# A fused LoRA kernel: 62 of 64 tiles keep a place of their own, and one group's halves go through the engines in turn

## The chip, the cores and the metric

The kernel runs on one NeuronCore of a Trainium2 chip. The metric is the device time of one execution in microseconds (us); the three runs of the kernel before took 124.76, 124.80 and 125.47, median 124.8. A profile is taken of one further execution. Engines are named as in the profile: PE is TensorE (matmuls), PEld its weight loads, DVE is VectorE, ACT is ScalarE, POOL is GpSimd, and SP is SyncE, which here only issues DMA transfers. "Span" is the time from the first to the last instruction in the profile.

## The reference

```python
def setup_inputs():
    batch, seq, d_model, r = 16, 512, 768, 16
    # x: 16 x 512 x 768, A: 768 x 16, B: 16 x 768, all float32; scale = 0.5
...
def reference(x, A, B, scale):
    lora = np.matmul(np.matmul(x, A), B)
    return (x + scale * lora).astype(np.float32)
```

x has 8192 rows (tokens) of 768 numbers, 25.2 MB. Every row is read once, gets a small correction through a rank-16 bottleneck, and is written once. So 50.3 MB cross the memory bus, and A and B are tiny.

## The kernel before

**Tiles.** A tile is 128 tokens, one per partition of the on-chip memory, with 768 float32 each (3 KB per partition, 384 KB in all). There are 64 tiles. `PARTS` cuts them into transfers of 2, 6, 8, 16, 16 and 16 tiles. The on-chip memory holds x in three rooms of 16 tiles (`rooms`), 48 places in all. The tiles of the last part (number 5) are loaded over parts 0, 1 and 2, so they must wait until these have been stored; that load is cut in two halves of 8 tiles, each behind the stores that free its place.

**Groups.** Compute goes in 8 groups of 8 tiles (`GROUP`), each in two halves of 4 (`SUB`). For a group:

1. *Narrow* (line 167): ACT copies the first half to half precision (`xh`), POOL the second half. There are two buffers `xh[0]`, `xh[1]` of a whole group each.
2. *Turn* (line 237): DVE transposes 32 x 32 blocks of `xh` in place, one instruction per half. After that the channel dimension lies along the partitions in every block.
3. *Project* (line 270): PE multiplies by A. 24 matmuls of 128 x 256, with the weights `w_bd` (A repeated on a block diagonal) accumulate `y_ps`, the 16 numbers per token. There are two `y_ps` buffers.
4. *Spread* (line 201): ACT copies four 32-partition blocks of `y_ps`, times the scale, to the diagonal of `y_bd` (two buffers).
5. *Raise* (line 288): PE multiplies by B, a pair of tiles at a time, 4 matmuls per pair (columns 512, 256, 256, 512), into one of two `lora` accumulators.
6. *Add* (line 250): DVE adds a pair's `lora` to the float32 tiles in place.

**Order on the engines.** Every engine runs a program of its own, written inside a block (`nc.Block`, lines 130 to 317). PE's loop takes two groups per turn and weaves the raising of group g with the projection of group g+1 in thirds: raise pairs 0 and 1, project 8 matmuls, raise pair 2, project 8, raise pair 3, project 8. DVE turns both halves of group g+1 and then does the four additions of group g. At start-up DVE also builds `w_bd` from A (lines 216 to 231), and ACT narrows B (`b_half`), which PE spreads with a selection matrix `pick` and ACT copies back as `b_mm`. The scratch for that (`a_rows`, `a_t`, `w_one`, `b_rows`, `b_half`, `pick`) has memory of its own.

**Order of the transfers.** All transfers are issued by SP and run in one queue, in the order of their issue. SP issues the loads of parts 0 and 1, A, B, and parts 2, 3 and 4; then the stores of parts 0, 1 and 2, each once the additions of its groups are done (`s_sum`, which DVE signals after a drain); then the two halves of load 5, the first when the stores of parts 0 and 1 have landed, the second when the store of part 2 has; then the remaining stores.

```python
        for st, done in zip(STORES, (s_out0, s_out0, s_out1)):
            store(st, done)
        e.wait_ge(s_out0, 32)
        load(LOADS[5])
        e.wait_ge(s_out1, 16)
        load(LOADS[6])
        for st in STORES[3:]:
            store(st, s_out)
```

At the end POOL waits until the last stores have landed.

Of the kernel before, what the change touches and what calls it, by code (L numbers as in the profile page):

```python
# [13 lines left out]
PARTS = [2, 6, 8, 16, 16, 16]  # L14

ROOM = [(0, 0), (0, 2), (0, 8), (1, 0), (2, 0), (0, 0)]
# [10 lines left out]
def kernel(  # L27
# [31 lines left out]
    rooms = [sb(f"x_sb{i}", [P, 16, D], fp32) for i in range(3)]  # L59
# [4 lines left out]
    a_rows = sb("a_rows", [P, 64 * R], fp32)  # L64
    a_t = sb("a_t", [P, 2, R, Q], fp32)
    w_one = sb("w_one", [Q, NC, 2, R], MM_DT)
    b_rows = sb("b_rows", [P, D], fp32)
    b_half = sb("b_half", [P, D], MM_DT)
    pick = sb("pick", [P, NQ, Q], MM_DT)
    w_bd = sb("w_bd", [P, NC, 2, P], MM_DT)  # L70
    b_mm = sb("b_mm", [P, D], MM_DT)
    xh = [sb(f"xh{i}", [P, GROUP, D], MM_DT) for i in range(2)]
    y_bd = [sb(f"y_bd{i}", [P, GROUP, P], MM_DT) for i in range(2)]
    lora = [ps(f"lora_ps{i}", [P, 2, D]) for i in range(2)]
    y_ps = [ps(f"ps_yt{i}", [P, GROUP, Q]) for i in range(2)]
# [3 lines left out]
    def sem(name):  # L79
        sems.append(nc.alloc_semaphore(name))  # L80
        return sems[-1]

# [12 lines left out]
    def held(i, s, n):  # L95
        r, s0 = ROOM[i]
        return rooms[r][:, ds(s0 + s, n), :]


    LOADS = [(0, 0, 2), (1, 0, 6), (2, 0, 8), (3, 0, 16), (4, 0, 16), (5, 0, 8), (5, 8, 8)]  # L100
    s_load = {ld: sem(f"s_load{k}") for k, ld in enumerate(LOADS)}

    def load_sem(t):
        i, s = where[t]
        return next(s_load[ld] for ld in LOADS if ld[0] == i and ld[1] <= s < ld[1] + ld[2])

    s_a, s_b = sem("s_a"), sem("s_b")
    s_brows, s_pick, s_bh, s_bp = sem("s_brows"), sem("s_pick"), sem("s_bh"), sem("s_bp")
    s_ready, s_zero, s_bm = sem("s_ready"), sem("s_zero"), sem("s_bm")
    s_nact, s_npool = sem("s_nact"), sem("s_npool")  # L110
    s_turned, s_y, s_spread = sem("s_turned"), sem("s_y"), sem("s_spread")
    s_lora, s_sum = sem("s_lora"), sem("s_sum")

    s_free = [sem(f"s_free{p}") for p in range(PAIRS)]
    s_out0, s_out1, s_out = sem("s_out0"), sem("s_out1"), sem("s_out")

    MMS = 2 * NC
    THIRD = MMS // 3

    STORES = [(0, 0, 2), (1, 0, 6), (2, 0, 8), (3, 0, 16), (4, 0, 16), (5, 0, 8), (5, 8, 8)]  # L120


    def groups_for(i, s, n):
        return where.index((i, s + n - 1)) // GROUP + 1

    STORED = list(dict.fromkeys(groups_for(*st) for st in STORES))
# [3 lines left out]
    programs = ExitStack()  # L130
    block = programs.enter_context(nc.Block(no_gpsimd_drain=True))

    @block.sync
    def _(e):
        def load(ld):
            e.dma_start(out=held(*ld), in_=memory(x2, *ld)).then_inc(s_load[ld], 16)  # L136

        def store(st, done):
            e.wait_ge(s_sum, STORED.index(groups_for(*st)) + 1)
            e.dma_start(out=memory(out2, *st), in_=held(*st)).then_inc(done, 16)  # L140

        load(LOADS[0])
        load(LOADS[1])
        e.wait_ge(s_ready, 1)
        e.dma_start(  # L145
            out=a_rows[0 : NC * APART : APART, :], in_=A.rearrange("(c e) r -> c (e r)", e=64)
        ).then_inc(s_a, 16)
        e.wait_ge(s_brows, 1)
        e.dma_start(out=b_rows[0 : R * APART : APART, :], in_=B).then_inc(s_b, 16)  # L149
        for ld in LOADS[2:5]:  # L150
            load(ld)
        for st, done in zip(STORES, (s_out0, s_out0, s_out1)):
            store(st, done)
        e.wait_ge(s_out0, 32)
        load(LOADS[5])
        e.wait_ge(s_out1, 16)
        load(LOADS[6])
        for st in STORES[3:]:
            store(st, s_out)

    def narrowed(e, copy, done, g, q):
        t = g * GROUP + q * SUB
        for s in dict.fromkeys(load_sem(t + k) for k in range(SUB)):
            e.wait_ge(s, 16)
        if q and g >= 2:
            e.wait_ge(s_y, g - 1)
        copy(  # L167
            out=xh[g % 2][:, ds(q * SUB, SUB), :], in_=held(*where[t], SUB)
        ).then_inc(done, 1)

    @block.gpsimd
    def _(e):
        e.memset(a_rows[0 : NC * APART], 0.0).then_inc(s_ready, 1)  # L173
        e.memset(b_rows, 0.0).then_inc(s_brows, 1)  # L174

        e.sem_inc(s_spread, 1)
        for s in s_free[2:]:
            e.sem_inc(s, 1)
        e.memset(pick, 0.0).then_inc(s_pick, 1)
        e.memset(w_bd.rearrange("p c k m -> p (c k m)").bitcast(fp32), 0.0)  # L180
        for t in y_bd:
            e.memset(t.rearrange("p s m -> p (s m)").bitcast(fp32), 0.0)  # L182
        e.wait_ge(s_pick, 1)
        e.affine_select(  # L184
            out=pick, in_=pick, compare_op=mybir.AluOpType.not_equal, fill=1.0, base=0,
            pattern=[[0, NQ], [-APART, Q]], channel_multiplier=1,
        ).then_inc(s_zero, 1)
        for g in range(NG):
            narrowed(e, e.tensor_copy, s_npool, g, 1)

    @block.scalar
    def _(e):
        e.wait_ge(s_zero, 1)
        e.wait_ge(s_b, 16)
        e.copy(out=b_half, in_=b_rows).then_inc(s_bh, 1)  # L195

        def spread(g):
            e.wait_ge(s_y, g + 1)
            for b in range(NQ):
                q = ds(b * Q, Q)  # L200
                last = e.mul(out=y_bd[g % 2][q, :, q], in_=y_ps[g % 2][q, :, :], mul=sc)  # L201
            last.then_inc(s_spread, 1)

        narrowed(e, e.copy, s_nact, 0, 0)
        e.wait_ge(s_bp, 1)
        e.copy(out=b_mm, in_=lora[0][:, 0, :]).then_inc(s_bm, 1)  # L206
        narrowed(e, e.copy, s_nact, 1, 0)
        for g in range(NG):
            spread(g)
            if g + 2 < NG:  # L210
                narrowed(e, e.copy, s_nact, g + 2, 0)

    @block.vector
    def _(e):
# [13 lines left out]
        e.wait_ge(s_ready, 3)  # L228
        e.wait_ge(s_zero, 1)
        for b in range(NQ):  # L230
            e.tensor_copy(out=w_bd[ds(b * Q, Q), :, :, ds(b * Q, R)], in_=w_one)  # L231

        def turned(g):
            for q, s in ((0, s_nact), (1, s_npool)):
                e.wait_ge(s, g + 1)
                v = xh[g % 2][:, ds(q * SUB, SUB), :].bitcast(fp32)
                last = e.transpose(out=v, in_=v)  # L237
            last.then_inc(s_turned, 1)

        turned(0)  # L240
        for p in range(PAIRS):
            e.wait_ge(s_lora, p + 1)
            e.sem_inc(s_free[p], 1)
        for g in range(NG):
            if g + 1 < NG:
                turned(g + 1)
            for p in range(PAIRS):
                xs = held(*where[g * GROUP + 2 * p], 2)
                e.wait_ge(s_lora, (g + 1) * PAIRS + p + 1)
                ins = e.tensor_tensor(  # L250
                    out=xs, in0=xs, in1=lora[p % 2], op=mybir.AluOpType.add
                )
                if g + 1 < NG or p + 2 < PAIRS:
                    ins.then_inc(s_free[p], 1)
                elif p + 1 == PAIRS:
                    ins.then_inc(s_sum, 1)
            if g + 1 in STORED[:-1]:
                e.drain().then_inc(s_sum, 1)  # L258

    @block.tensor  # L260
    def _(e):


        def projected(h, steps):
            if steps[0] == 0:
                e.wait_ge(s_turned, 1)
            xv = xh[h].rearrange("p s (c j k) -> p s c j k", c=NC, k=2)
            for m in steps:
                c, k = divmod(m, 2)
                last = e.matmul(  # L270
                    y_ps[h], w_bd[:, c, k, :], xv[:, :, c, :, k],
                    start=(m == 0), stop=(m == MMS - 1),
                )
            if steps[0] == 0:
                last.then_inc(s_turned, -1)
            elif steps[-1] == MMS - 1:
                last.then_inc(s_y, 1)

        def raised(h, p):
# [6 lines left out]
            for k in range(2):  # L286
                for n0, w in ((0, 512), (512, 256)) if k == 0 else ((0, 256), (256, 512)):
                    mms.append(e.matmul(  # L288
                        t[:, k, ds(n0, w)], y_bd[h][:, 2 * p + k, :], b_mm[:, ds(n0, w)],
# [4 lines left out]
            mms[1].then_inc(free, -1)  # L294
            mms[-1].then_inc(s_lora, 1)
# [9 lines left out]
        with e.Fori(0, NG // 2):  # L305
            for h in range(2):
                raised(1 - h, 0)
                raised(1 - h, 1)
                projected(h, range(0, THIRD))
                raised(1 - h, 2)  # L310
                projected(h, range(THIRD, 2 * THIRD))
                raised(1 - h, 3)
                projected(h, range(2 * THIRD, MMS))
        for p in range(PAIRS):
            raised(1, p)

    programs.close()  # L317
    nums = [s.num for s in sems]
    assert nums == list(range(nums[0], nums[0] + len(nums))) and sems[-1] is s_out
    nc.gpsimd.sem_clear(range(nums[0], nums[-1]))  # L320
    nc.gpsimd.wait_ge(s_out, 4 * 16)
    nc.gpsimd.sem_inc(s_out, -4 * 16)
# [36 lines left out]
```

## Time and profile before

| | |
|---|---|
| median of three runs | 124.8 us (124.76 to 125.47) |
| the profiled execution's own time | 124.78 us |
| its span | 122.8 us |
| bytes read and written | 25.26 MB and 25.17 MB |
| share of the span in which the 16 DMA engines were busy | 96.7% |
| busiest compute engine: DVE | 85.4 us, 70% of the span |
| PE / ACT / POOL | 47% / 30% / 22% |
| mean granted PE clock | 0.873 |

How to read it: the page of the profile gives shares over the whole span, a strip of 40 slices (each 3.07 us) with the busy tenths of every engine, the granted PE clock and the DMA rate, and then the costliest groups of instructions by line. "Idle before" is the time an engine stood still ahead of instructions of that group, and the arrow names what ended it. The timeline lists instructions in order, with runs of the same instruction merged; its first two columns are the start and the length, in us from the span's start. The profiled execution took 124.78 us, 2.0 more than its span, so a change in the span stands beside the median of 124.8 one to one.

### The profile page before, as it was taken

To read this page: it belongs to the slowest core of one execution; us is meant where nothing else is said; L and a number is where in the kernel's file an instruction comes from. 1 tells how busy PE (TensorE), PEld (TensorE's weight loads), DVE (VectorE), ACT (ScalarE), POOL (GpSimd) and SP (SyncE) were. 2 spreads that over 40 slices of the span, in tenths; PEclk is the share of its full clock that TensorE was granted. 3 is DMA by queue.
4 is the path that set the end of the run, shared out by engine and by line. 5 is a ranking of instruction groups with operands and counts; after the bars stand their busy time and mean duration, and the time that the engine had idled before them with its cause. 6 is when DMAs were issued, how large, how long until landed. Compare 5 with 4: busy or idle time off the path is not lost.

```text
span 122.8 us, 920 instructions
## 1 busy us (share of the span) xinstructions
PE 58.1 (47%) x338; PEld 33.5 (27%) x338; DVE 85.4 (70%) x56; ACT 36.8 (30%) x43; POOL 26.4 (22%) x19
## 2 busy tenths in 40 slices
PE   0000239948907944694584389449439645000000
PEld 0000015625503632362252145235224322000000
DVE  0004984089969999989999998999999859600000
ACT  0002958040199141707604080840400310000000
POOL 7703508000196001707100080440000000000000
PEclk9999999999995999769999958999995999655555
DMA  3999999799799895999999999899799799899990
GB/s 104 434 444 402 424 528 464 304 512 480 304 496 496 384 400 222 466 448 400 480 400 448 440 392 528 384 480 464 336 496 451 336 496 464 344 432 408 472 424 32
DMA packets 2073, 50.44 MB, mean 411 GB/s; under 512 B 252, under 2 KB 252, under 8 KB 536
## 3 DMA queue, kind: packets, MB, share of 16 engines
q1 hardware_dynamic: 2072, 50.43, 96.7%
q14 instruction: 1, 0.01, 0.0%
HBM read 25.26 MB, written 25.17 MB: 411 GB/s over the span
## 4 chain that ended last, share of the span: by engine, by line
DVE 40%; DMA 24%; PE 10%; DVEq 5%; ACT 2%; issue 2%; SPq 2%; POOL 1%; POOLq 0%
DMA x_sb<-in_x_dram 24%; DVE x_sb L250 23%; DVE xh L237 17%; PE lora_ps L288 6%; PE ps_yt L270 4%; DVEq L258 4%; ACT xh L167 2%; DVEq L317 1%; POOL a_rows L173 1%; SPq L145 1%; SPq L136 1%; SPq L149 0%; POOLq L354 0%; SPq L129 0%
## 5 line engine op out<-in xcount | busy, mean ns | idle before, releaser
L250 DVE TENSOR_TENSOR x_sb<-x_sb,lora_ps 128x1536 f32<-128x1536 f32 x32 | 54.0, 1738 | 2.6 <-PE lora_ps L288 2.6
L288 PE MATMUL lora_ps<-b_mm,y_bd 128*128 128x512 f16 (+1 forms) x144 | 33.0, 369 | 23.5 <-ACT y_bd L201 9.2
L167 POOL CAST xh<-x_sb 128x3072 f16<-128x3072 f32 x8 | 21.9, 2746 | 54.0 <-DMA x_sb<-in_x_dram 49.3
L270 PE MATMUL ps_yt<-xh,w_bd 128*128 128x256 f16 x192 | 28.9, 297 | 8.6 <-DVE xh L237 8.6
L237 DVE STREAM_TRANSPOSE xh<-xh 128x1536 f32<-128x1536 f32 x16 | 27.5, 1756 | 7.1 <-PE lora_ps L288 5.2
L167 ACT CAST xh<-x_sb 128x3072 f16<-128x3072 f32 x8 | 22.0, 2751 | 14.1 <-DMA x_sb<-in_x_dram 14.0
L270 PEld LDWEIGHTS ps_yt<-xh,w_bd 128*128 128x128 f16 x192 | 19.8, 106 | 18.0 <-DVE xh L237 10.9
L288 PEld LDWEIGHTS lora_ps<-b_mm,y_bd 128*128 128x128 f16 x144 | 13.5, 105 | 38.3 <-issue 24.1
L201 ACT ACTIVATE y_bd<-ps_yt 32x256 f16<-32x256 f32 x32 | 12.0, 374 | 36.1 <-PE ps_yt L270 35.8
L216 DVE STREAM_TRANSPOSE a_t<-a_rows 96x1024 f32<-96x1024 f32 x1 | 1.9, 1926 | 11.0 <-DMA a_rows<-in_A_dram 11.0
L299 PE MATMUL lora_ps<-b_half,pick 128*128 128x512 f16 (+1 forms) x2 | 0.8, 515 | 13.7 <-ACT b_half L195 13.7
L195 ACT ACT_TABLE_LOAD x1 | 1.3, 1283 | 11.6 <-DMA b_rows<-in_B_dram 11.6
L299 PEld LDWEIGHTS lora_ps<-b_half,pick 128*128 128x128 f16 x2 | 0.1, 112 | 13.7 <-ACT b_half L195 13.7
L223 DVE CAST w_one<-a_t 32x128 f16<-32x128 f32 x3 | 1.7, 573 | 0.1
L180 POOL MEMSET w_bd<- 128x1536 f32 x1 | 1.4, 1378 | 0.0
L173 POOL MEMSET a_rows<- 96x1024 f32 x1 | 0.9, 947 | 0.5 <-SPq L129 0.5
L231 DVE COPY w_bd<-w_one 32x384 f16<-32x384 f16 x4 | 1.0, 250 | 0.1
L182 POOL MEMSET y_bd<- 128x512 f32 x2 | 1.0, 521 | 0.0
L195 ACT CAST b_half<-b_rows 128x768 f16<-128x768 f32 x1 | 0.8, 831 | 0.0
L206 ACT CAST b_mm<-lora_ps 128x768 f16<-128x768 f32 x1 | 0.8, 798 | 0.0
L174 POOL MEMSET b_rows<- 128x768 f32 x1 | 0.7, 735 | 0.0
L184 POOL TENSOR_SCALAR_AFFINE_SELECT pick<-pick 128x128 f16<-128x128 f16 x1 | 0.3, 306 | 0.0
(5 smaller groups left out, 0.6 us busy)
## 6 DMA issues: line engine op xcount, KB each, us to landing
x_sb<-in_x_dram SPq DMA_DIRECT2D x2, 6144.0 KB, 36.5
out_dram<-x_sb SPq DMA_DIRECT2D x2, 6144.0 KB, 23.0
x_sb<-in_x_dram SPq DMA_DIRECT2D x3, 3072.0 KB, 15.1
out_dram<-x_sb SPq DMA_DIRECT2D x3, 3072.0 KB, 16.6
x_sb<-in_x_dram SPq DMA_DIRECT2D x1, 2304.0 KB, 9.9
out_dram<-x_sb SPq DMA_DIRECT2D x1, 2304.0 KB, 20.4
x_sb<-in_x_dram SPq DMA_DIRECT2D x1, 768.0 KB, 4.5
out_dram<-x_sb SPq DMA_DIRECT2D x1, 768.0 KB, 15.4
```

What stands on the lines that cost most here:

```text
L167: copy(out=xh[g % 2][:, ds(q * SUB, SUB), :], in_=held(*where[t], SUB)).then_inc(done, 1)
L173: e.memset(a_rows[0 : NC * APART], 0.0).then_inc(s_ready, 1)
L180: e.memset(w_bd.rearrange("p c k m -> p (c k m)").bitcast(fp32), 0.0)
L195: e.copy(out=b_half, in_=b_rows).then_inc(s_bh, 1)
L201: last = e.mul(out=y_bd[g % 2][q, :, q], in_=y_ps[g % 2][q, :, :], mul=sc)
L216: e.transpose(out=a_t[0 : NC * APART].rearrange("i k r c -> i (k r) c"), in_=a_rows[0 : NC * APART].rearrange("c (i k r) -> c (k r) i", k= ...
L223: last = e.tensor_copy(out=w_one[:, ds(b * EACH, EACH), :, :], in_=a_t[ds(b * Q, Q)].rearrange("i k r (c n) -> i c k r n", n=APART)[..., 0],)
L237: last = e.transpose(out=v, in_=v)
L250: ins = e.tensor_tensor(out=xs, in0=xs, in1=lora[p % 2], op=mybir.AluOpType.add)
L258: e.drain().then_inc(s_sum, 1)
L270: last = e.matmul(y_ps[h], w_bd[:, c, k, :], xv[:, :, c, :, k], start=(m == 0), stop=(m == MMS - 1),)
L288: mms.append(e.matmul(t[:, k, ds(n0, w)], y_bd[h][:, 2 * p + k, :], b_mm[:, ds(n0, w)], start=True, stop=True,))
```

## The change

- **Places.** 62 tiles have a place of their own in one buffer `x_all`; `PARTS` is now 2, 6, 8, 16, 16, 14, 2. Only the last two tiles (part 6) are loaded over the first two. Load 5 (14 tiles) no longer waits for stores.
- **Scratch.** The start-up scratch lies inside the room of part 5. So SP waits for the first projection (`s_y`) before it issues load 5.
- **Order of SP.** Load 5 is issued ahead of all stores. After the stores of parts 0 and 1 are issued, SP waits until store 0 has landed, issues load 6, and goes on with the stores.
- **When a store is issued.** Before: after a drain on DVE that follows the group's additions. Now: PE signals `s_sum` with the third matmul of its second pair in each round, and the store of group g (counted from 0) waits for round g+2. PE comes there when the spread of group g+1 is done and the group's fourth addition has freed its accumulator. The last two stores wait for DVE's last addition (`s_last`).
- **Halves in turn.** One `xh` buffer per half (4 tiles), one `y_bd`, one `y_ps`. A half is narrowed when the projection of the same half of the group before is done. PE projects a half at a time with 24 matmuls of 128 x 128 (48 per group in place of 24 of 128 x 256). Its loop is one group: raise pairs 0 and 1, project half 0, raise pairs 2 and 3, project half 1. DVE turns one half, adds two pairs, turns the other half, adds two pairs.
- **ACT** now copies A's weights to the diagonal of `w_bd` (four copies of 32 x 384 that DVE did), after `b_mm`; PE waits for that before its loop.
- **No blocks.** The engines' programs are written straight into the kernel. POOL clears semaphores in two steps at the end.

```diff
-PARTS = [2, 6, 8, 16, 16, 16]
-ROOM = [(0, 0), (0, 2), (0, 8), (1, 0), (2, 0), (0, 0)]
+PARTS = [2, 6, 8, 16, 16, 14, 2]
...
-    rooms = [sb(f"x_sb{i}", [P, 16, D], fp32) for i in range(3)]
+    ROOM = sum(PARTS[:-1])
+    x_all = sb("x_sb", [P, ROOM, D], fp32)
+    spare = x_all[:, ds(ROOM - PARTS[-2], PARTS[-2]), :].rearrange("p s d -> p (s d)")
...
-    xh = [sb(f"xh{i}", [P, GROUP, D], MM_DT) for i in range(2)]
-    y_bd = [sb(f"y_bd{i}", [P, GROUP, P], MM_DT) for i in range(2)]
+    xh = [sb(f"xh{h}", [P, SUB, D], MM_DT) for h in range(2)]
+    y_bd = sb("y_bd", [P, GROUP, P], MM_DT)
...
-    y_ps = [ps(f"ps_yt{i}", [P, GROUP, Q]) for i in range(2)]
+    y_ps = ps("ps_yt", [P, GROUP, Q])
...
+    def tiles(t, n):
+        return x_all[:, ds(t % ROOM, n), :]
...
-        for ld in LOADS[2:5]:
-            load(ld)
-        for st, done in zip(STORES, (s_out0, s_out0, s_out1)):
-            store(st, done)
-        e.wait_ge(s_out0, 32)
-        load(LOADS[5])
-        e.wait_ge(s_out1, 16)
-        load(LOADS[6])
-        for st in STORES[3:]:
-            store(st, s_out)
+        for i in range(2, len(PARTS) - 2):
+            load(i)
+        e.wait_ge(s_y, 1)
+        load(len(PARTS) - 2)
+        for st in STORES:
+            i, s, n = st
+            groups = where.index((i, s + n - 1)) // GROUP + 1
+            if groups < NG:
+                e.wait_ge(s_sum, groups + 2)
+            else:
+                e.wait_ge(s_last, 1)
+            ins = e.dma_start(out=memory(out2, *st), in_=held(*st))
+            ins.then_inc(s_out if i else s_out0, 16)
+            if i == 1:
+                e.wait_ge(s_out0, 16)
+                load(len(PARTS) - 1)
...
-        if q and g >= 2:
-            e.wait_ge(s_y, g - 1)
+        if g:
+            e.wait_ge(s_y, 2 * g + h - 1)
...
+        e.wait_ge(s_ready, 3)
+        for b in range(NQ):
+            last = e.copy(out=w_bd[ds(b * Q, Q), :, :, ds(b * Q, R)], in_=w_one)
+        last.then_inc(s_w, 1)
...
         for g in range(NG):
-            if g + 1 < NG:
-                turned(g + 1)
-            for p in range(PAIRS):
...
-            if g + 1 in STORED[:-1]:
-                e.drain().then_inc(s_sum, 1)
+            for h in range(2):
+                if g + 1 < NG:
+                    turned(g + 1, h)
+                summed(g, 2 * h)
+                summed(g, 2 * h + 1)
...
+            for m in range(MMS):
                 c, k = divmod(m, 2)
-                last = e.matmul(
-                    y_ps[h], w_bd[:, c, k, :], xv[:, :, c, :, k],
+                mm = e.matmul(
+                    y_ps[:, ds(h * SUB, SUB), :], w_bd[:, c, k, :], xv[:, :, c, :, k],
...
+            if p == 1:
+                mms[2].then_inc(s_sum, 1)
             mms[-1].then_inc(s_lora, 1)
...
-        with e.Fori(0, NG // 2):
+        with e.Fori(0, NG):
             for h in range(2):
-                raised(1 - h, 0)
-                raised(1 - h, 1)
-                projected(h, range(0, THIRD))
-                raised(1 - h, 2)
-                projected(h, range(THIRD, 2 * THIRD))
-                raised(1 - h, 3)
-                projected(h, range(2 * THIRD, MMS))
+                raised(2 * h)
+                raised(2 * h + 1)
+                projected(h)
```

## The prediction

> **What bounds the kernel now.** First the page's head, the slices and the queues:
>
> ```profile
> span 122.8 us, 920 instructions
> ...
> PE 58.1 (47%) x338; PEld 33.5 (27%) x338; DVE 85.4 (70%) x56; ACT 36.8 (30%) x43; POOL 26.4 (22%) x19
> ...
> DMA  3999999799799895999999999899799799899990
> GB/s 104 434 444 402 424 528 464 304 512 480 304 496 496 384 400 222 466 448 400 480 400 448 440 392 528 384 480 464 336 496 451 336 496 464 344 432 408 472 424 32
> ...
> q1 hardware_dynamic: 2072, 50.43, 96.7%
> ```
>
> The transfers fill the span: 16 engines busy 96.7% of 122.8 = 118.7 us. The first load is issued at 0.97 and moves data from about 2.0; the last landing recorded is at 121.9. So of 119.9 us of possible transfer only about 1.2 are empty. No compute engine is near that. The chain of waits names DVE (40%) ahead of DMA (24%), but it follows issues, not the queue; so I read next when SP issued (timeline of SP) and how long a store took to land:
>
> ```profile
> 35.11 11.38 SPq L140 DMA_DIRECT2D out_dram<-x_sb  x3
> 55.95 7.66 SPq L136 DMA_DIRECT2D x_sb<-in_x_dram  x2
> 66.87 39.81 SPq L140 DMA_DIRECT2D out_dram<-x_sb  x4
> ```
> ```profile
> DMA to landing us min/median/max: 15.4/17.1/26.0
> ```
>
> A store of 2 tiles took 15.4 us because it stood behind 48 tiles of loads. The 16-tile store issued at 66.9 took the 26.0 and landed at 92.9. The two 16-tile stores have a median of 23.0, so the next took 20.0; issued at 87.4 (end of that group's additions), it landed at 107.4. 16 tiles thus cost 14.5 us. Compute ends at 106.3 (last row of DVE), 15.6 ahead of the last landing: the queue had work waiting all along. **The bound is the DMA queue, and it only moves if the queue runs dry, starts later or moves bytes more slowly.** One hole shows, in 1 us windows (columns: PE, PEld, DVE, ACT, POOL, clock, DMA share, GB/s):
>
> ```profile
> 45.00:46.00 1.00, 0.00 (x0) 0.00 (x0) 1.00 (x1) 0.98 (x3) 0.00 (x0) 1.00 1.16 344
> 46.00:47.00 1.00, 0.81 (x5) 0.51 (x6) 0.86 (x2) 0.09 (x1) 0.00 (x0) 1.00 0.00 0
> 47.00:48.00 1.00, 0.65 (x5) 0.20 (x2) 1.00 (x2) 0.00 (x0) 0.00 (x0) 1.00 0.51 209
> ```
>
> There the queue turns from the last load of 48 KB rows to the first store, although that store was issued at 35.1. Rows are counted where they start; the last load's rows took about 0.9 us longer than others. The turns at 63 and 78 show no such hole.
>
> **The change, part by part.**
>
> *Places and order of SP.* Bytes are the same. Loads of 62 tiles run first; load 5 waits for the first projection, some 24 us, and is needed in the queue only when 48 tiles are through, at 48: nothing waits. Then come stores 0 and 1 (8 tiles), load 6 (2), store 2 (8), store 3 (16), store 4 (16), and the rest. SP waits for store 0's landing with store 2 queued behind it on SP; store 1's 6 tiles cover that (6 x 0.91 = 5.5 us against an issue of 0.4 and 1.0 to first data, which the first load took from 0.97 to 2.0). Load 6 lands near 70 and is read near 88. So what can go wrong is a store issued too late. Store 3 starts when 80 tiles are through, store 4 when 96 are; before, 80 were through at 78.4 (second half of load 5, row of ACT) and 96 at 92.9. Less 1.1 us from issue to data, **store 3 is due by 77.3 and store 4 by 91.8**; each us later is a us on the end. The later ones are due by 106 and 113. The hole may come at either turn from loads to stores: the sum takes one of 0.9 as before, the range none to two.
>
> *Start-up.* ACT makes the four `w_bd` copies that DVE made (0.25 each). No row has 32x384 on ACT; between 0.374 (32x256, L201) and 0.80 (768, L206) by elements: 0.48, four 1.9. `b_mm` ends at 17.1, so PE starts at 19.05, not 17.4. Its clock is cold: 8 raising matmuls took 2.5 (17.39 to 19.90), to 21.6. Then projection 0.
>
> *The price of a 128-column matmul* is the unknown:
>
> ```profile
> L270 PE MATMUL ps_yt<-xh,w_bd 128*128 128x256 f16 x192 | 28.9, 297 | 8.6 <-DVE xh L237 8.6
> L270 PEld LDWEIGHTS ps_yt<-xh,w_bd 128*128 128x128 f16 x192 | 19.8, 106 | 18.0 <-DVE xh L237 10.9
> L201 ACT ACTIVATE y_bd<-ps_yt 32x256 f16<-32x256 f32 x32 | 12.0, 374 | 36.1 <-PE ps_yt L270 35.8
> ```
>
> Eight with 256 columns took 1.05 us, one lasts 0.27, so they start (1.05 - 0.27) / 7 = 0.111 apart; cold, (1.91 - 0.42) / 7 = 0.213. The spacing doubles with the halved clock, so columns set it, and half the columns would be 0.056. The other end is no gain, 0.111, if a weight load (mean 0.106) must fit between two starts; but two loads took 0.14 together (PEld at 17.35), so loads overlap. I take 0.056, a half 24 x 0.056 + 0.16 = 1.5 us; at 0.111 it is 2.8. [...] No row here has 128 columns.
>
> So projection 0 ends near 24.0 (cold until about 23.4, as before), raising pairs 2 and 3 takes 1.3 (16 x 0.16 / 2), projection 1 ends at 26.6; before, 25.7. Spread 1.53 + 0.1, first pair raised 0.85 later: first addition at 29.2, before 28.3.
>
> *Steady state.* From there two loops compete. DVE per group, from its timeline:
>
> ```profile
> 77.33 3.43 DVE L237 STREAM_TRANSPOSE xh<-xh 128x1536 f32<-128x1536 f32 x2
> 80.68 6.71 DVE L250 TENSOR_TENSOR x_sb<-x_sb,lora_ps 128x1536 f32<-128x1536 f32 x4
> ```
>
> From 77.33 to 87.39: 10.06, the same six instructions after the change; the drains (0.14 each) and waits of 0.3 to 0.4 in every second group go, 10.3 to 10.06. The other loop, from the end of projection 1 of a group: spread 1.63, raise 0.85, two additions 3.35, turn 1.7, start 0.05, projection 1.5 = 9.1. DVE's own work covers it by 1.0; with 2.8 it would be 10.4, and the halves with single buffers would set the pace. POOL's narrowing (2.75) runs beside spread, raise and additions (5.8).
>
> Additions of group g start at 29.2 + 10.06 g and end 8.4 later; round g+2 then raises pair 0 (0.65 to its last start) and reaches the third matmul of pair 1 0.6 later: its store goes at 38.9 + 10.06 g. **Store 3 (g = 3): 69.1, due 77.3. Store 4 (g = 5): 89.2, due 91.8. Margin 2.6 us.** Before, they went at 66.9 and 87.4. Last additions near 105.5; due 113.
>
> *No blocks.* SP's first issue at 0.97 follows the barrier at 0.80; a branch less may save up to 0.1. At the end one more clearing of semaphores, between 0.02 (a semaphore step now) and 0.2 (the clearing at 107), costs about 0.1. Together nothing.
>
> *Clock.* Windows of 3.41 us with PE busy 1.34 (47.25 to 50.66, and 67.73 to 71.14) were followed by half clock, those with 1.74 not. After the change the thinnest is about 1.4, on the edge: a halved window costs a projection 1.3 and a raised pair 0.6, less the cover of 1.0, so about 0.7 (half of 1.3 + 0.6 + 0.5 left over) in at most two groups up to store 4: 90.6, still in time. [...]
>
> **Sum:** span 122.8 + 0 (queue) + 0 (ends) = 122.8; with 2.0 around it 124.8, the median of before.
>
> **Rivals.**
> 1. *Projection sets the pace (slower).* Place: 128-column matmuls bound by weight loads; decides from a spacing of about 0.10. At 0.111: start-up 1.5 later, groups 10.4, store 4 at 89.2 + 1.5 + 5 x 0.38 = 92.6 to 93.2 with waits between, 0.8 to 1.4 late: 125.6 to 126.2. At the mean 1.05/8 = 0.131 a half is 3.3, groups 10.9, start-up 2.5 later: 95.9 to 96.6, 4 to 5 late: 129 to 129.6. For: weight loads of 106 per 128 columns. Against: the overlapping loads and the cold spacing. 0.17.
> 2. *Late stores by thin margin*: a start-up 2 us longer with a halved clock in every second group: 89.2 + 2 + 2 = 93.2: 1.4 late, 126.2. 0.08.
> 3. *Turns cost otherwise.* 14-tile rows leave no hole: 123.9; or a hole at both turns (load 5 to store 0, load 6 to store 2): 125.7. 0.15.
> 4. *The change does what it says and gains*: loads free of stores would help only were compute waiting for load 5. POOL and ACT wait for the halves at 70.5 and 78.4, but DVE is busy there. Gain by compute ending earlier: none, 15.6 us of stores stand behind it. A gain over 1% needs the hole and 0.4 more: 0.05, near 123.4.
>
> Forecast 0.55. One per cent (1.25 us) is about what a measurement of this kernel can tell from no change. Faster by more 0.05; within 0.71 (forecast, rival 3, 0.01 of rival 1); slower 0.24 (rivals 1 and 2). Range 123.7 to 126.9: it takes in rival 3 on both sides, rival 2 and the lower part of rival 1, and leaves out its upper part and a gain.
>
> **What would show it.** Right: DMA slices full to the end; 16-tile stores issued near 69 and 89; 128-column matmuls about 0.056 apart; DVE without idle time from 29. Wrong: a slice of low GB/s ahead of store 4 near 92; PE's waits of DVE replaced by DVE waiting for PE `lora_ps`; a last landing far from 121.9 with no dry slice, which would mean that transfers themselves changed their speed.

## The result, and the profile after

The changed kernel takes 125.11 us (median of 22 runs, 124.85 to 127.03) against 124.75 for the kernel before (22 runs, 124.40 to 125.47). The ratio is 1.0034, with a 95% interval of 1.0019 to 1.0050: slower by a third of a per cent, 0.36 us on the medians. Medians are of all runs; the ratios leave out runs that lie more than 1.5% above the fastest of their kernel. The time lies in the forecast range and within the 1% called "same"; but 124.8 meant no change, and there is a small one, clear of noise.

Most of what the prediction worked out inside the span came out as written. The page of the profile after, head and main groups:

```profile
span 122.7 us, 1317 instructions
...
PE 56.3 (46%) x530; PEld 37.1 (30%) x530; DVE 83.9 (68%) x52; ACT 38.7 (32%) x47; POOL 26.2 (21%) x19
...
DMA  3999998899799699999599999899796996898994
...
q1 hardware_dynamic: 2216, 50.43, 96.8%
...
L260 PE MATMUL ps_yt<-xh,w_bd 128*128 128x128 f16 x384 | 26.4, 226 | 8.2 <-DVE xh L230 8.2
L201 ACT COPY w_bd<-x_sb 32x384 f16<-32x384 f16 x4 | 2.0, 508 | 0.0
```

The transfers fill 96.8% of the span (96.7% before). The timeline of DVE, where its steady state begins:

```profile
29.39 3.42 DVE L235 TENSOR_TENSOR x_sb<-x_sb,lora_ps 128x1536 f32<-128x1536 f32 x2 [0.57 <-PE lora_ps L277]
32.72 1.77 DVE L230 STREAM_TRANSPOSE xh<-xh 128x1536 f32<-128x1536 f32 x1
34.41 3.38 DVE L235 TENSOR_TENSOR x_sb<-x_sb,lora_ps 128x1536 f32<-128x1536 f32 x2
37.72 1.76 DVE L230 STREAM_TRANSPOSE xh<-xh 128x1536 f32<-128x1536 f32 x1
```

The first addition starts at 29.39 (predicted 29.2), DVE has no gap from there to 89, and a group takes 9.98 us (34.41 to 44.39 in the timeline; predicted 10.06). On PE, a half's projection in the warm state:

```profile
34.64 1.54 PE L260 MATMUL ps_yt<-xh,w_bd 128*128 128x128 f16 x24 [0.95 <-DVE xh L230]
...
84.52 2.51 PE L260 MATMUL ps_yt<-xh,w_bd 128*128 128x128 f16 x24 [0.95 <-DVE xh L230]
88.70 2.72 PE L277 MATMUL lora_ps<-b_mm,y_bd 128*128 128x512 f16 x8 [1.67 <-issue]
```

24 matmuls take 1.54 us and one lasts 0.217, so they start (1.54 - 0.217) / 23 = 0.058 apart; 0.056 was taken. The other two rows show what did not go as planned: from 84.79 to 91.61 the granted clock is 0.50. That is 6.83 us, two windows of 3.41 in a row, where each of the four halvings ahead of 100 us in the kernel before lasted 3.41. Projection and raising take 2.5 and 2.7 in place of 1.5 and 1.5. That is just ahead of the store of part 4. Its issue, and what the DMA engines did (timeline of SP; then windows, the last two columns are DMA share and GB/s):

```profile
91.02 0.33 SPq L157 DMA_DIRECT2D out_dram<-x_sb  x1
```
```profile
90.20:91.20 1.00, 1.00 (x4) 0.44 (x3) 1.00 (x1) 0.00 (x0) 0.00 (x0) 0.50 0.01 0
91.20:92.20 1.00, 1.00 (x15) 0.98 (x14) 1.00 (x2) 0.00 (x0) 0.00 (x0) 0.79 1.86 786
92.20:93.20 1.00, 1.00 (x16) 0.87 (x14) 1.00 (x1) 0.00 (x0) 0.00 (x0) 1.00 0.00 0
```

The store went at 91.02; predicted were 89.2, and 90.6 with a halved clock. The windows count rows of 48 KB where they start, so an empty window alone proves nothing. Following the ends of rows to the next starts in the packet records, in order of time (the records do not name the engine), the 16 engines stood dry for 0.68 us on the mean, about 1.1 at most, all near 91. In this execution it cost nothing: the first engine ended its last row of the store before at 90.81, but the last one only at 92.00 (landing at 92.36), when data had been coming again since 91.86, and the last landing is at 121.76 (121.91 before).

So this execution's span is 0.14 *shorter* than before and its time 0.07 *longer*. What grew lies around the span: 124.85 - 122.685 = 2.17 us, against 124.78 - 122.826 = 1.95. From the last landing to the end of the span it is 0.93 and 0.92, so the two-step clearing added nothing that counts. The profile has one view on that stretch, the DMA queues after the last store, of the kernel before and then of the changed one:

```profile
q8 instruction: 1, 0.02, 1.8%
```
```profile
q14 instruction: 2, 0.02, 1.6%
```

The view gives their kind as *instruction*: fetches of instructions, one of 16 KB at 124.03 before, two of 8 KB at 123.32 and 124.35 after, the second 1.67 us behind the end of the span.

Two theories came out of this. *Dry queue*: the store of part 4 comes late when the clock is halved, and each us beyond about 90 to 91 is a us on the end. *Fetch*: without blocks, the programs lie differently in what is fetched, and an engine that leaves the kernel waits for a fetch. This was a guess: the records give a fetch's queue, size, start and length, and not whose it is. The rival to both was that transfers or the two-step clearing cost the 0.36.

### The profile page after: what moved, and what is told of

Its sections match the earlier page's. It is cut to its first block, busy times and chain, and to the rows that moved or that the text cites. A ratio compares the mean times of both kernels' runs of the same rounds, so it can differ in the third digit from the quotient of the medians.

```text
span 122.7 us, 1317 instructions
## 1 busy us (share of the span) xinstructions
PE 56.3 (46%) x530; PEld 37.1 (30%) x530; DVE 83.9 (68%) x52; ACT 38.7 (32%) x47; POOL 26.2 (21%) x19
## 3 DMA queue, kind: packets, MB, share of 16 engines
q1 hardware_dynamic: 2216, 50.43, 96.8%
## 4 chain that ended last, share of the span: by engine, by line
DVE 54%; PE 12%; DMA 7%; ACT 6%; issue 5%; POOL 1%; SPq 1%; POOLq 0%; ACTq 0%
DVE x_sb L235 38%; DVE xh L230 16%; DMA x_sb<-in_B_dram 7%; PE ps_yt L260 6%; PE lora_ps L277 6%; ACT xh L171 2%; ACT w_bd L201 2%; ACT y_bd L209 1%; POOL x_sb L175 1%; SPq L139 1%; ACT x_sb L195 1%; ACT b_mm L198 1%; ACT L195 0%; POOLq L349 0%; SPq L129 0%
## 5 line engine op out<-in xcount | busy, mean ns | idle before, releaser
L277 PE MATMUL lora_ps<-b_mm,y_bd 128*128 128x512 f16 (+1 forms) x144 | 30.3, 348 | 25.5 <-ACT y_bd L209 10.0
L171 POOL CAST xh<-x_sb 128x3072 f16<-128x3072 f32 (+1 forms) x9 | 22.1, 2465 | 63.1 <-PE ps_yt L260 56.6
L260 PE MATMUL ps_yt<-xh,w_bd 128*128 128x128 f16 x384 | 26.4, 226 | 8.2 <-DVE xh L230 8.2
L260 PEld LDWEIGHTS ps_yt<-xh,w_bd 128*128 128x128 f16 x384 | 24.4, 100 | 13.5 <-issue 13.1
L277 PEld LDWEIGHTS lora_ps<-b_mm,y_bd 128*128 128x128 f16 x144 | 12.7, 101 | 39.0 <-issue 21.9
L214 DVE STREAM_TRANSPOSE x_sb<-x_sb 96x1024 f32<-96x1024 f32 x1 | 1.9, 1933 | 11.2 <-DMA x_sb<-in_A_dram 11.2
L290 PE MATMUL lora_ps<-x_sb 128*128 128x512 f16 (+1 forms) x2 | 0.8, 514 | 13.7 <-ACT x_sb L195 13.7
L201 ACT COPY w_bd<-x_sb 32x384 f16<-32x384 f16 x4 | 2.0, 508 | 0.0
L221 DVE CAST x_sb<-x_sb 32x128 f16<-32x128 f32 x3 | 1.5, 508 | 0.1
L175 POOL MEMSET x_sb<- 96x1024 f32 x1 | 0.9, 948 | 0.5 <-SPq L129 0.5
```

Source lines behind the costliest of these rows:

```text
L171: last = copy(out=xh[h][:, ds(k, n), :], in_=tiles(t + k, n))
L201: last = e.copy(out=w_bd[ds(b * Q, Q), :, :, ds(b * Q, R)], in_=w_one)
L214: e.transpose(out=a_t[0 : NC * APART].rearrange("i k r c -> i (k r) c"), in_=a_rows[0 : NC * APART].rearrange("c (i k r) -> c (k r) i", k= ...
L221: last = e.tensor_copy(out=w_one[:, ds(b * EACH, EACH), :, :], in_=a_t[ds(b * Q, Q)].rearrange("i k r (c n) -> i c k r n", n=APART)[..., 0],)
L260: mm = e.matmul(y_ps[:, ds(h * SUB, SUB), :], w_bd[:, c, k, :], xv[:, :, c, :, k], start=(m == 0), stop=(m == MMS - 1),)
L277: mms.append(e.matmul(t[:, k, ds(n0, w)], y_bd[:, 2 * p + k, :], b_mm[:, ds(n0, w)], start=True, stop=True,))
```

## The experiments

### The changed kernel again, and the store of part 4 cut in two

> The changed kernel unaltered, for a second profile and a reference within this call. Theory (dry queue): the last 8 of 16 tiles of the store before were being written when SP issued the 16-tile store of part 4 at 91.0, so the engines stood 0.7 us dry; the issue moves with the granted PE clock from run to run. Expected: 125.1, ratio to the kernel before 1.002 to 1.005, and a dry stretch ahead of that store whose size follows its issue time. Rival (ends and turns): the same time whatever the issue time is.

```diff
-        (0, 0, 2), (1, 0, 6), (2, 0, 8), (3, 0, 16), (4, 0, 16), (5, 0, 8), (5, 8, 6), (6, 0, 2)
+        (0, 0, 2), (1, 0, 6), (2, 0, 8), (3, 0, 16), (4, 0, 8), (4, 8, 8), (5, 0, 8), (5, 8, 6), (6, 0, 2)
```

> The 16-tile store of part 4 is cut in two of 8; the first half is issued a group earlier, near 79, so the queue holds 7.3 us more when the second comes near 91. Theory (dry queue): no dry stretch near 91, and 0.3 to 0.7 us faster than the changed kernel, 124.4 to 124.8. Rival (the ends, the two-step clearing, the transfers and their turns cost the 0.36): 125.1 as before the edit, or more for one transfer added.

The unaltered kernel: 125.83 (12 runs, 124.85 to 126.94), ratio 1.0045 (1.0021 to 1.0069). Its profiled execution, 126.81, is one of the upper ones, and its trace shows where the time went. The store of part 4 goes at 93.01, within three windows of half clock from 86.4 to 96.7; the timeline of SP and the windows:

```profile
93.01 0.33 SPq L157 DMA_DIRECT2D out_dram<-x_sb  x1
```
```profile
91.00:92.00 1.00, 1.00 (x5) 0.53 (x4) 0.19 (x1) 0.00 (x0) 1.00 (x1) 0.50 0.01 0
92.00:93.00 1.00, 1.00 (x5) 0.53 (x4) 0.83 (x1) 0.00 (x0) 0.06 (x1) 0.50 0.00 0
93.00:94.00 1.00, 1.00 (x9) 0.80 (x8) 1.00 (x2) 0.00 (x0) 0.00 (x0) 0.50 1.85 786
```

The engines stand dry for 2.6 us on the mean, and the last landing is at 123.71: 1.99 later in the issue and 1.95 later in the landing than in the first profile. What lies around the span is the same, 2.17. The lateness does not come from these windows alone: the full clock is first on record at 25.00 in place of 23.35 (where, in the first profile, the 128-column matmuls go from 0.107 to 0.057 us apart), so the first addition started at 30.13 in place of 29.39, and a halving from 45.5 to 52.3 cost DVE another 0.96.

With the store cut in two the spread of the runs is gone: 125.12 (11 runs, 124.92 to 125.25), ratio 1.0019 (1.0003 to 1.0034). In its profile the clock is halved from 85.3 to 95.6, and the second half of the store goes at 91.98, later than in the first profile, yet no engine runs dry. But the median stays, and so does the stretch around the span (2.20). So the dry queue can account for runs from 125.7 upward (4 of 22, then 7 of 12 for the unaltered kernel; shown in the one that was profiled), and not for the ordinary run at 125.1. In all eleven it is the span that is longer, 123.6 to 124.9, and not what lies around it, 2.13 to 2.24. I had put all of the 0.36 on it; that was wrong.

### DVE's signal for the stores

```diff
+            if g + 1 < NG:
+                e.drain().then_inc(s_sum, 1)
...
-                e.wait_ge(s_sum, groups + 2)
+                e.wait_ge(s_sum, groups)
...
-            if p == 1:
-                mms[2].then_inc(s_sum, 1)
```

> The store's signal comes from DVE after a drain when the group's additions are done, as in the kernel before, and no longer from PE's second pair two rounds later. Theory (dry queue): the store of part 4 goes near 88 in place of 89 to 91, and no longer depends on a halved PE clock; due by 90.0 for the first engine to run out; 124.4 to 124.8. Cost: seven drains of 0.14 on DVE, which has idle time to spare behind it. Rival (ends and turns): 125.1.

124.75 (11 runs, 124.65 to 124.79), ratio 0.9991 (0.9977 to 1.0005): as fast as the kernel before. The store of part 4 goes at 89.51 in its profile; the clock was not halved ahead of it, so this profile does not show whether the signal shields the store from the clock. But this could not be the store alone: the last landing, 122.06, is no earlier than with the split store (122.02). Time less span is 1.77, and one of the two fetches now falls at 105, under the transfers. The seven drains also make DVE's program longer by seven instructions.

### A fuller PE

```diff
                 projected(h)
+            for _ in range(4):
+                e.matmul(idle_ps, w_bd[:, 0, 0, :], b_mm[:, 0:512], start=True, stop=True)
```

> Four matmuls of 512 columns on constant operands, into a bank that nobody reads, stand after the projection of half 1 in every round, 0.86 us in the 1.67 us in which PE waits for the spread. Theory (dry queue, made late by the halved clock): no window of half clock between 24 and 95, store 4 issued near 89.2, and 124.5 to 124.9. If the late issue had nothing to do with the clock: 125.1 or more. Rival (ends and turns): 125.1.

125.34 (10 runs, 125.09 to 125.96), ratio 1.0048 (1.0027 to 1.0069). The edit missed its aim: the clock is still halved from 84.6 to 88.0. It does not tell the theories apart as it was meant to, but its profile shows the ordinary loss without a dry queue: 125.09, store of part 4 at 90.01, no engine dry, last landing 122.00, time less span 2.17.

### Seven bare drains; the blocks put back

Both on the kernel with the split store, so that no queue runs dry.

```diff
                 summed(g, 2 * h + 1)
+            if g + 1 < NG:
+                e.drain()
```

> The store of part 4 cut in two as in the run with the split store (125.12, no dry stretch, 2.20 us between span and time, two instruction fetches after the span), and seven bare drains on DVE that signal nothing, at the places where the run with DVE's signal had its drains (124.75, 1.77 between span and time, one fetch after the span and one at 105). Theory (fetch): the drains move DVE's program by seven instructions, so that one fetch of 8 KB falls under the transfers; 124.7, and 1.8 around the span. Rival (DVE's signal itself gave the 0.37): 125.1, and 2.2 around the span.

```diff
-    on_sync(nc.sync)
...
-    on_tensor(nc.tensor)
+    with nc.Block(no_gpsimd_drain=True) as block:
+        block.sync(on_sync)
...
+        block.tensor(on_tensor)
```

> The store of part 4 cut in two, and the program blocks put back around the engines' programs; nothing else. Theory (fetch): what lies around the span depends on how the programs lie in their fetched pages; with blocks 1.8 to 2.0 in place of 2.2, so 124.7 to 124.9. Rival (the blocks are worth nothing, as I predicted): 125.1, 2.2 around the span.

The drains that do nothing give 124.82 (12 runs), ratio 0.9989 (0.9972 to 1.0007), 1.80 around the span. The blocks give 124.75 (12 runs), ratio 0.9994 (0.9981 to 1.0007), and 1.62 around it. Spans are 123.0 and 123.1, *longer* than with the split store alone (122.9). In both, one fetch lies behind the span where two did; the queue's line for the split store and for the seven drains:

```profile
q14 instruction: 2, 0.02, 1.5%
```
```profile
q14 instruction: 1, 0.01, 1.0%
```

So the steady part of the loss is neither in the stores nor in the transfers (the last landings, 122.12 and 122.06, are no earlier than 122.02 with the split store alone), nor in the two-step clearing, which these kernels keep. It goes with the programs: seven more instructions on DVE, or the blocks, take 2.20 around the span to 1.80 or 1.62.

### The blocks put back in the changed kernel alone

> The changed kernel with the program blocks put back and nothing else, so the store of part 4 may still come late. Theory (two causes that add up): one fetch after the span, 1.6 to 1.8 around it, lowest runs near 124.5, and still runs of up to 126.5 where the clock is halved ahead of store 4; median 124.75 to 125.3. If the fetch alone made the change slower: all runs within 124.6 to 125.0.

124.83 (12 runs, 124.73 to 126.52), ratio 0.9993 (0.9962 to 1.0023), 1.62 around the span. Eleven runs lie between 124.73 and 125.08, and one at 126.52. The blocks take the steady 0.3 away. The excess of the one high run lies in its span (124.9), as a late store would have it, but it was not the profiled one, so that is not shown.

### The store of part 4 held back a round

```diff
-                e.wait_ge(s_sum, groups + 2)
+                e.wait_ge(s_sum, groups + (3 if i == 4 else 2))
```

> The changed kernel with the store of part 4 held back one round more, to about 99.9 in place of 89 to 91. Theory (dry queue): each us beyond 90.0, when the first engine has written all of the store before, is a us on the end: data from 101.0, 32 tiles at 0.91 after it, last landing 130.2, time 133.0 (within 0.5). Rival (the end does not hang on this store, compute or the ends set it): well under 130.

132.23 in one run, 0.8 under the 133.0 expected and so outside its 0.5: the clock was never halved ahead of this store, which went at 98.49 and not at 99.9. From 98.49 the theory would have given 131.6, so it is 0.6 short; half of that lies behind the last landing (3.10, where 2.8 was taken). The windows of this kernel (the last column is GB/s):

```profile
91.00:93.00 2.00, 1.16 (x7) 0.31 (x4) 2.00 (x2) 0.00 (x0) 0.00 (x0) 1.00 0.00 0
93.00:95.00 2.00, 1.05 (x19) 1.03 (x19) 2.00 (x2) 0.00 (x0) 0.00 (x0) 1.00 0.00 0
95.00:97.00 2.00, 0.54 (x10) 0.37 (x7) 2.00 (x2) 1.39 (x4) 0.00 (x0) 1.00 0.00 0
97.00:99.00 2.00, 1.46 (x8) 0.71 (x8) 1.10 (x2) 0.11 (x1) 0.00 (x0) 1.00 0.00 0
99.00:101.00 2.00, 0.82 (x4) 0.31 (x4) 2.00 (x2) 0.00 (x0) 0.00 (x0) 1.00 0.94 393
```

Issued 7.47 us later than in the first profile, the last landing (129.13) is 7.37 later. So a us of lateness cost 0.99 us. In this profile the store of part 3 went at 68.56; two groups of 9.98 later is 88.5, where the unaltered store of part 4 would have gone at full clock, near the 89.2 predicted.

### Where the fetch comes from

On the kernel with the split store, bare drains stand behind the end of one or more programs:

```diff
+        for _ in range(2):        # DVE, behind its last addition; 40 in the second
+            e.drain()
```

> The split store and two bare drains at the end of DVE's program, behind its last addition and under the transfers. What is compared is the time less the span, which was 2.17 to 2.20 in all five profiles of programs without blocks whose DVE had 61 instructions, 1.77 to 1.80 in the three with seven more. Theory (the page of DVE's program ends within a few instructions of its end, and the fetch behind the span of the next page costs 0.37): either still 2.17 with two fetches behind the span, or 1.80 with one, nothing between. Rival (the drains in the loop did something else): 2.17 with one fetch, or 1.80 with two.

> The same with forty drains. Theory: 1.80 around the span, one fetch behind it and one near 105. Rival (seven drains within the loop changed the time otherwise, not the place of the program's end): 2.17.

> The split store and twelve drains at the end of the programs of ACT, POOL, SP and PE, none on DVE. Theory: the other fetch moves under the transfers, DVE's stays behind the span, and the time around the span stays at 2.17, because DVE's is the one that ends last. Rival (any fetch behind the span costs): below 2.0.

| kernel (one profiled execution each) | time - span | time - last landing | instruction fetches after the last store (start less the span's end) |
|---|---|---|---|
| split store | 2.20 | 3.12 | +0.66, +1.97 |
| + 12 drains on ACT, POOL, SP and PE | 2.20 | 3.11 | +1.66 |
| + 2 drains on DVE's end | 1.94 | 2.86 | +0.64, +1.11 |
| + 40 drains on DVE's end | 1.77 | 2.69 | +0.67 |
| + 7 drains in DVE's loop | 1.80 | 2.72 | +0.67 |
| + blocks | 1.62 | 2.69 | +0.65 |

The late fetch goes with DVE's program: with drains on the other four engines only the early one is gone, and 2.20 stays 2.20; two drains on DVE bring the late one to +1.11, and with forty none is left there. Two drains gave a value in between, which I had excluded: the fetch is not either there or not, it starts earlier, and the time around the span is 1.94. Why it starts earlier is not shown; nor does any view show where a program lies in what is fetched, so the pages of the expectations are my conjecture. That the length of DVE's program counts is thus shown, by twelve runs for the seven drains and by one each for the others. That DVE stands still for the fetch is argued, not shown: no view has its instructions behind the span, and +1.66 and +1.97 go with the same 2.20.

The blocks fit into this row. With them the span itself ends 1.07 behind the last landing in place of 0.92, which makes time less span look better by 0.15; counted from the last landing, they give what DVE's drains give, and one fetch is left where two were. That they work by the same way is not shown separately.

The counter-test, twelve drains at the ends of other programs:

> DVE's signal and the load of part 5 in two transfers (124.70, one fetch left after the span), and twelve bare drains at the end of the programs of ACT, POOL, SP and PE, under the last transfers. If the fetch that is left belongs to one of these engines and its page ends within twelve instructions, it moves under the transfers: 124.3, 1.4 around the span. If not: 124.7; or 125.0, if an engine that was clear of a page's end is pushed over one.

> The kernel before with twelve bare drains at the end of PE's program. Behind its span lies one fetch of 16 KB in a queue of its own (1.0 us long). If that is PE's next page and ends within twelve instructions of the program: 124.4 and 1.6 around the span. If not: 124.8.

On the kernel with DVE's signal and short rows they take the last fetch away: none is left behind the span, and 1.80 stays 1.80 (124.94, 12 runs, ratio 1.0009, 0.9981 to 1.0038). Three of these runs lie between 125.67 and 126.11 although DVE gives the signal. Their spans are ordinary (123.0 to 123.2), and 2.57 to 3.11 lies around them, against 1.75 to 1.83 in the other nine; so not every high run is a late store of part 4, and what else makes them stays open. On the kernel before, twelve drains on PE move the 16 KB fetch to 108 and leave 2.02 in place of 1.95 (125.15, ratio 1.0009, 0.9989 to 1.0028). One profile says little here: over 97 runs of the kernel before, taken beside the other kernels, time less span goes from 1.89 to 2.52 with 1.98 in the middle, and the twelve runs with the drains on PE lie between 1.98 and 2.09. Without the late 16 KB fetch the value spreads less and is no lower. So the count of fetches does not set the time; of the fetches that were moved, only the one that goes with DVE's program came with another time.

### Shorter rows ahead of the turn

```diff
-        load(len(PARTS) - 2)
+        for s, n in ((0, 8), (8, 6)):
+            ld = (5, s, n)
+            e.dma_start(out=held(*ld), in_=memory(x2, *ld)).then_inc(s_load[5], 16)
```

> DVE's signal (124.75), and load 5 in two transfers of 8 and 6 tiles, so that the last rows read before the first store are 18 KB long and not 42 KB. Theory (the hole at the turn scales with the row in flight): the rows before the turn are stretched by 0.2 in place of 0.8 us per engine, time 124.1 to 124.3. Rival (a fixed cost of a turn): stretched by 0.6 to 0.9 in all and 124.75.

> The kernel before, with load 4 (16 tiles, rows of 48 KB) in two transfers of 8 tiles. The same two theories of the hole at 46: by row length 0.9 falls to about 0.4, 124.3; by a fixed cost of a turn 124.75.

At the turn from loads to stores, rows of 42 KB are stretched by 0.81 us per engine with DVE's signal (0.59 in the first profile, 0.6 to 0.9 over all profiles with such rows), and rows of 18 KB by 0.44 (124.70, 12 runs, ratio 0.9986, 0.9973 to 0.9999, against 124.75 with DVE's signal alone). In the kernel before, 48 KB rows lose 0.90 and 24 KB rows 0.68 (125.00, 0.9996, 0.9972 to 1.0020). The loss shrinks with the row, but less than in proportion and by hardly more than it varies between executions, and the gain in time is at most 0.1: mostly a price of the turn. DVE's signal with short rows is the fastest kernel here, by 0.15 us on the medians against the kernel before measured beside it (124.85), with an interval that just leaves out no change.

## Why the prediction was right and wrong

- **The bound is the DMA queue; compute runs under it.** Right. First addition, group time, matmul spacing (0.058, taken 0.056), `w_bd` copies (0.51, taken 0.48), the store of part 3 (69.05, taken 69.1) and last landing are within 0.3 us or a few per cent.
- **"Span 122.8 + 0 + 0."** Right in this execution to 0.14, in part by luck: the queue did run dry ahead of the store of part 4, by 0.68 us on the mean, which the sum had at nothing, and the time by which the 16 engines had drifted apart (90.81 to 92.00) took it up.
- **"With 2.0 around it."** Here the forecast failed. The step took what lies around the span as a constant that a change carries along. Nor does a change in the span then stand beside the median one to one, as the section on the time before has it. For the changed kernel it is nearly constant (2.12 to 2.23 over the 22 runs), but at another value: 1.95 before, 2.17 after in the profiles. For the kernel before it is no constant at all (1.89 to 2.52, with 1.98 in the middle).
- **"No blocks: together nothing."** Failed for the same reason. I priced a branch at the start and a clearing at the end, which indeed came to nothing (first issue at 0.97 in both, span's end 0.01 later behind the last landing), and not that the length of DVE's program counts after the span (2.20 to 1.80 with seven more instructions). Putting the blocks back alone takes 2.17 to 1.62, and from the last landing 3.09 to 2.69. Of the 0.36 us on the medians, about 0.2 is around the span; the rest is the span of an ordinary run (122.9 to 123.0 in most of the 22) and the late runs, which I cannot divide further, since profiles of the kernel before and of light edits to it have spans of 122.83 to 123.15.
- **"Clock: at most two groups, 90.6, still in time."** A halving came, and its size was off. I let single windows of half clock fall in between groups and charged 0.7 each. Two or three windows came in a row, and because PE gives the signal for the store, they also stretch the way from the fourth addition to the issue: from 87.67 to 91.02, 3.35 us, against about 1.3 planned. The start-up moves with the clock too, which I had at full from 23.4 as a constant: it is first on record at full at 22.2 to 25.1 in the profiles of the changed kernel and its variants. The store went at 91.0 and 93.0. Nor does PE's busy time in a window tell which halvings come. In the profile after, PE was busy for 1.63 us of the 3.42 ahead of the halving at 84.79, and for 2.24 in the half-clock window from there to 88.20, which a second one followed; four windows with 1.54 (from 43.83, 54.07, 64.31 and 95.03) were followed by full clock. PE's longest gap ahead of 84.79 was the 1.67 us that every group has from 36 on, halved or not; in the kernel before it was 2.07 at most ahead of three of the four halvings.
- **"Due by 91.8."** I took a landing (92.9) less 1.1. In the profile after, the 16 engines ended their last rows of the store before between 90.81 and 92.00, and data came 0.84 after the issue; so the store was due at 90.0 for the first engine and at 91.2 for the last. An issue at 91.02 cost nothing, one at 93.01 cost 1.7 against an undisturbed landing at 122.0 (of the split store), where 91.8 gives 1.2 and 91.2 gives 1.8. Rival 2, the late store, thus is real in a part of the runs, with the parts it named, a longer start-up and a halved clock, both of them from the clock. Rival 1 is not (0.058), and neither is rival 3: one turn stretches its rows, by 0.6 to 0.9, as the sum had it.

## What to carry to other kernels

Where one transfer queue is the bound, list for each transfer when the queue will reach it and when it is issued, by the first engine that runs out and not the last, and take the signal from the engine that finishes the data, not from one behind it whose clock can be halved (here PE, at 0.50 from 84.79 to 91.61). A store of 16 tiles cut in two is cheap insurance (runs of 124.92 to 125.25, where the uncut store had 124.85 to 126.94). And before a few tenths of a us are put down to an idea, compare time less span over several runs, since one profile can mislead (the kernel before: 1.89 to 2.52): if it moved, look for instruction fetches behind the last instruction, and try bare drains at the ends of the programs, which moved them here.

## What the runs showed that I had not expected

- Time less span lay between 1.62 and 2.20 us by program in the profiles. For the changed kernel it kept to 2.17, whether its execution took 124.85, 126.81 or, with one store held back, 132.23; for the kernel before it spread over 0.6 us.
- Where the 8 KB fetch that goes with DVE's program starts 1.1 us behind the span's end, the time is about 0.15 us longer; where it starts 1.7 to 2.0 behind it, about 0.4; where it lies under the transfers, no longer. Why the kernel before has 2.87 from the last landing, and 2.94 with no fetch left behind its span, in place of 2.69, stays open.
- After 0.7 us of dry queue the last store's 16 parts land within 0.3 us of each other, where they land 1.5 to 1.9 us apart in a queue that never runs dry. In the profile after, the engines ended their rows ahead of the pause between 90.81 and 92.00 and began again between 91.86 and 92.10: the late ones caught up, and the issue at 91.02, 1.0 behind the 90.0 of the first engine, cost nothing.
